# Eight more seven-product pairs in the down projections of an fp32 decoder trunk

## The chip, the core and the metric

The kernel runs on one core of one Trainium2 chip. The metric is device time in microseconds (us) of one execution. A core has a matrix engine (PE), whose weight loads (PEld) run beside its matmuls, a vector engine (DVE), a scalar engine (ACT), a general engine (POOL), and a sync engine (SP) that here does nothing but start DMA transfers. The 16 DMA engines of the core are shared by all queues; a transfer is started by SP or by POOL.

## The reference, cut to what matters

The reference is a decoder trunk of two layers on 256 tokens with D = 2048, all in float32. Layer 0 mixes tokens with gated linear attention, layer 1 with block-sparse attention. Each is followed by the same channel mixer:

```python
def conv_ffn(x, norm_w, w_up, conv_w, conv_b, w_down):
    S = x.shape[1]
    h = rms_norm(x, norm_w) @ w_up                 # 2048 -> 2 x 5632
    hp = jnp.pad(h, ((0, 0), (CONV_WIDTH - 1, 0), (0, 0)))
    acc = conv_b
    for j in range(CONV_WIDTH):
        acc = acc + conv_w[j] * hp[:, j:j + S]     # causal depthwise conv, width 3
    a, u = jnp.split(acc, 2, axis=-1)
    return (jax.nn.silu(a) * u) @ w_down           # 5632 -> 2048
...
    for layer in range(DEPTH):
        ...                                        # h = h + token mixer
        h = h + conv_ffn(h, ffn_norm[layer], ffn_w_up[layer], ffn_conv_w[layer],
                         ffn_conv_b[layer], ffn_w_down[layer])
```

The change touches the up projection (`@ w_up`, with the convolution and the gate), and above all the down projection (`@ w_down`), in both layers.

## The kernel before, in words

**Products.** Every float32 weight tile is split into two reduced-precision parts, whi (a rounded copy, ACT, line 143) and wlo (the rest, DVE, line 145); the activations are split in the same way. A product is three matmul passes: hi by hi, lo by hi, hi by lo.

**The weight stream.** `WeightStream` brings the weights once, as "halves" of 128 x 1024 floats (512 KB). SP starts each load (line 109) into one of 10 raw buffers (names wraw and ahead); ACT and DVE turn a half into one of 4 whi and 4 wlo buffers; PE uses it. In the down projections loads are started at most 10 halves ahead of the split, in the up projections 7. A raw buffer comes free when its half has been split.

**Up projection.** 22 groups of 8 steps, a step being one half and 12 matmuls. Behind each group ACT, DVE and POOL transpose the result, apply the convolution and the gate and split the hidden rows (`turn_up`, `conv`, `gate`). Some operand sums are made here too (below), and `make_ahead` forms sums of down-projection weights ahead of time: it loads two halves of w_dn into two raw buffers, does four DVE additions, and POOL stores both to DRAM ("parked" in tsum, line 339). It does so every 9 steps.

**Down projection.** `down` (lines 820 to 890) walks over two column blocks b of 1024 output columns. In each it takes 22 pairs; a pair is 256 of the 5632 hidden rows. The order of the pairs in a block is written out by hand in `ORDERS`, a table of one string for each layer and block; block 0 of both layers has the string `FIRST`. A plain number is a regular pair: two halves, eight products, 24 matmuls. A number with + or ^ is a seven-product pair, a Strassen-like scheme: 21 matmuls in place of 24. It needs sums of weights and sums of hidden rows as operands. Its weights come as one half of 256 KB, one of 512 KB and two parked halves of 512 KB, 1792 KB in all; with ^ the parked halves are loaded into long-lived slots (name sums) of the pool `big`, which has 32 slots, instead of the raw buffers. The last regular pairs of a block are its tail. Before, 58 pairs of 88 have seven products: 13 in block 0 of both layers, 15 and 17 in block 1 of layers 0 and 1.

**Operand sums of hidden rows.** A seven-product pair needs four sums ("combinations") of its hidden rows, each split in two; three of them are 384 KB. They are kept in `big` slots called comb; one slot has four quarters, so that three slots hold a fourth pair's sums in their last quarters. Three ways lead there: pairs 1 and 3 (EARLY) are made in the up projection and stay; the seven pairs of ASIDE are made in the up projection and put aside to DRAM (`put_aside`, lines 743 to 749, stored by POOL, line 748), and fetched back by POOL (`take_back`, line 751, DMA line 753) in block 0 of the down projection; the other pairs' sums are made in the down projection by DVE and ACT (`combine_parts`, line 755: one 128 x 512 addition, four 128 x 128 additions and the splits, lines 436 and 437). `MADE` gives for each pair the place in the block's order at which it is fetched or made. A pair's sums made in block 0 serve block 1 as well.

**What sets the order.** Each engine works through its own queue in program order. SP's loads follow the order of the halves and wait for a free raw buffer; POOL's queue holds copies for the last up-projection groups, then the fetches, then reloads of the residual stream (h, line 983, in layer 0; res, line 936, in layer 1).

Of the kernel before, what the change touches and what calls it, by code (L numbers as in the profile page):

```python
# [37 lines left out]
def _order(text):  # L38
# [117 lines left out]
def trunk(ctx: ExitStack, tc: tile.TileContext, xT, cst, msk, w1p, w2a, w_k, w_qa, w_v2, w_v, w_gt, w_g, w_got, w_go,  # L156
# [14 lines left out]
    def slot(shape, dt, name):  # L171
        return big.tile(shape, dt, name=name, tag="slot")
# [287 lines left out]
    make_ahead(0, w_dn0, 24, 9)  # L460
# [244 lines left out]
    combos, rooms_of = {}, {}  # L705
# [3 lines left out]
    def room(k, hid_k, kept):  # L709


        n = len(combos)
        if n % 4 < 3:
            rooms.append(slot([128, 4, 2, 128], F32R, "comb"))
            combos[k] = [(rooms[-1][:, f, 0], rooms[-1][:, f, 1]) for f in range(3)]
        else:
            combos[k] = [(c[:, 3, 0], c[:, 3, 1]) for c in rooms[-3:]]
        combos[k].append((hid_k[:, 0, 128:S], hid_k[:, 0, S + 128:]) if kept else
                         (rooms[-1][:, 3, 0], rooms[-1][:, 3, 1]))
        return rooms[-1] if n % 4 < 3 else None  # L720
# [99 lines left out]
    def down(layer, hid, ready, jobs):  # L820

        sevens = [{k for k, seven in order if seven} for order in ORDERS[layer]]
        done = set(EARLY)
        for b, order in enumerate(ORDERS[layer]):
            new = [k for k, seven in order if seven and k not in done]
            done |= set(new)
            todo = dict(jobs.get(b, {}))
            for k in MADE:
                if k not in new:
                    continue  # L830
                kept = k in sevens[-1]
                at, lag = MADE[k] if isinstance(MADE[k], tuple) else (MADE[k], 0)
                if lag:
                    todo.setdefault(at, []).append(
                        lambda k=k, kept=kept: rooms_of.update({k: room(k, hid[k], kept)}))
                todo.setdefault(at + lag, []).append(
                    (lambda k=k: take_back(layer, k, hid[k])) if k in ASIDE else
                    (lambda k=k, kept=kept: combine_parts(k, hid, kept)))
# [289 lines left out]
    make_ahead(1, w_dn1, 6, 9)  # L1128
# [157 lines left out]
```

## Time and profile before

| | us |
|---|---|
| median of three runs | 2169.53 |
| lowest and highest | 2169.51 and 2169.84 |
| the profiled execution, its own time | 2170.52 |
| its span (first to last instruction) | 2168.8 |
| PE busy in the span | 2160.1 |
| DVE, ACT, POOL busy | 1749.0, 1535.0, 351.5 |

Times inside the trace run from the span's start. The down projections lie, roughly, at 865 to 974 and 974 to 1092 us (layer 0, blocks 0 and 1) and at 1946 to 2055 and 2055 to 2165 us (layer 1); the up projections at 385 to 865 and 1466 to 1946 us. The share of the DMA engines is a mean over the 16 of the time that packets were under way; the GB/s beside it is what they moved. The granted clock of PE shows 9 (90% or more of 2.4 GHz) in all 40 slices of the page.

### The profile page before, as it was taken

Reading aid. Unit: us, or ns where it says so; the run is one execution under the profiler, and the core shown is the slowest. Engines: PE = TensorE matmul, PEld = TensorE weight load, DVE = VectorE, ACT = ScalarE, POOL = GpSimd, SP = SyncE. Lnnn points to the kernel's source line nnn. Section 1 sums busy time; section 2 is a strip of 40 time slices with the busy share of each in tenths; the row PEclk is TensorE's granted clock in tenths of the full one; section 3 lists DMA queues with packets and bytes.
Section 4 is the critical chain, followed back from the end, with each engine's and each line's share of the span. In section 5 each row is a group of like instructions: output and inputs, shape, how many; then the busy total and the mean of one; then the engine's idle time right before and its main releaser. Section 6 shows DMA issues by size and latency. Waiting matters only on the chain.

```text
span 2168.8 us, 30105 instructions
## 1 busy us (share of the span) xinstructions
PE 2160.1 (100%) x9936; PEld 1801.4 (83%) x9936; DVE 1749.0 (81%) x2525; ACT 1535.0 (71%) x2448; POOL 351.5 (16%) x519
## 2 busy tenths in 40 slices
PE   9999999999999999999999999999999999999999
PEld 7888888888888888888888888888888888888887
DVE  7676788778788887988977787587887888779898
ACT  6655554698899886767656575456888898967575
POOL 0000347100000004300002343150000000043000
PEclk9999999999999999999999999999999999999999
DMA  9586678978888886897968898779888888869996
GB/s 333 192 280 211 233 270 268 338 261 274 295 279 302 289 274 205 317 338 273 403 215 283 278 311 288 249 236 317 276 292 299 283 299 293 269 202 337 335 355 259
DMA packets 193600, 613.11 MB, mean 283 GB/s; under 512 B 38257, under 2 KB 38785, under 8 KB 193442
## 3 DMA queue, kind: packets, MB, share of 16 engines
q1 hardware_dynamic: 166322, 523.78, 71.1%
q0 software_dynamic: 26400, 86.60, 10.7%
q8 instruction: 78, 1.28, 0.2%
q10 hardware_dynamic: 720, 0.79, 0.1%
q14 instruction: 80, 0.66, 0.1%
HBM read 535.31 MB, written 75.78 MB: 282 GB/s over the span
## 4 chain that ended last, share of the span: by engine, by line
PE 99%; DMA 0%; DVE 0%; POOL 0%; issue 0%; SPq 0%; ACT 0%; POOLq 0%
PE acc L385 46%; PE acc L388 23%; PE acc L857 15%; PE p L857 6%; PE acc L370 5%; PE acc L372 2%; DMA wraw<-w_v 0%; PE sT L607 0%; PE tr L1059 0%; PE s L1077 0%; PE z L513 0%; PE o L493 0%; PE s L1075 0%; PE oT L493 0%; DVE wlo L145 0%; PE oT L492 0%
## 5 line engine op out<-in xcount | busy, mean ns | idle before, releaser
L145 DVE TENSOR_TENSOR wlo<-wraw,whi 128x1024 fp32r<-128x1024 f32 (+1 forms) x788 | 927.3, 1188 | 316.9 <-ACT whi L143 267.0
L143 ACT CAST whi<-wraw 128x1024 fp32r<-128x1024 f32 (+1 forms) x788 | 792.1, 1015 | 445.8 <-PE acc L385 262.5
L385 PE MATMUL acc<-whi,xw 128*128 128x512 f32 x3520 | 873.9, 390 | 1.4 <-ACT whi L143 1.2
L385 PEld LDWEIGHTS acc<-whi,xw 128*128 128x128 f32 x3520 | 659.7, 188 | 138.5 <-ACT whi L143 1.6
L388 PE MATMUL acc<-wlo,xw 128*128 128x512 f32 x1760 | 472.3, 389 | 0.0
L388 PEld LDWEIGHTS acc<-wlo,xw 128*128 128x128 f32 x1760 | 330.2, 188 | 68.4
L398 ACT COPY up<-uT 32x256 f32<-32x256 f32 x608 | 245.4, 404 | 8.5 <-DVE uT L776 1.0
L339 POOL DMA_DIRECT2D tsum<-ahead x116 | 62.6, 540 | 967.0 <-DVE ahead L327 563.5
L857 PE MATMUL acc<-whi,hid 128*128 128x512 f32 x588 | 167.6, 390 | 0.0
L145 DVE TENSOR_TENSOR wlo<-ahead,whi 128x1024 fp32r<-128x1024 f32 x98 | 120.5, 1232 | 17.4 <-ACT whi L143 11.1
L143 ACT CAST whi<-ahead 128x1024 fp32r<-128x1024 f32 x98 | 102.5, 1053 | 41.3 <-PE acc L857 19.8
L385 PE MATMUL acc<-whi,xkv 128*128 128x512 f32 x512 | 129.7, 391 | 0.0
L857 PEld LDWEIGHTS acc<-whi,hid 128*128 128x128 f32 x588 | 110.1, 188 | 22.6
L857 PE MATMUL p<-whi,hid 128*128 128x512 f32 x356 | 112.1, 389 | 0.0
L385 PEld LDWEIGHTS acc<-whi,xkv 128*128 128x128 f32 x512 | 95.3, 188 | 18.9
L857 PE MATMUL acc<-whi,comb 128*128 128x512 f32 x348 | 101.3, 389 | 0.0
L857 PE MATMUL acc<-wlo,hid 128*128 128x512 f32 x294 | 96.2, 389 | 0.0
L789 ACT ACTIVATE au<-up,cs 128x256 f32<-128x256 f32 x176 | 95.7, 593 | 0.0
L398 POOL COPY up<-uT 32x256 f32<-32x256 f32 x96 | 72.2, 752 | 96.4 <-DVE uT L776 74.1
L796 DVE SCALAR_TENSOR_TENSOR au<-up,cs,au 128x254 f32<-128x254 f32 x176 | 80.7, 483 | 0.0
L326 DVE TENSOR_TENSOR ahead<-ahead 128x512 f32<-128x512 f32 x116 | 80.2, 691 | 0.0
L327 DVE TENSOR_TENSOR ahead<-ahead 128x512 f32<-128x512 f32 x116 | 79.7, 687 | 0.1
(283 smaller groups left out, 2409.2 us busy)
## 6 DMA issues: line engine op xcount, KB each, us to landing
wraw<-w_up SPq DMA_DIRECT2D x352, 512.0 KB, 5.9
wraw<-w_dn SPq DMA_DIRECT2D x118, 512.0 KB, 6.4
ahead<-w_dn SPq DMA_DIRECT2D x116, 512.0 KB, 6.1
tsum<-ahead POOLq DMA_DIRECT2D x116, 512.0 KB, 6.1
ahead<-tsum SPq DMA_DIRECT2D x98, 512.0 KB, 6.1
wraw<-w_mq SPq DMA_DIRECT2D x32, 512.0 KB, 5.9
wraw<-w_kk SPq DMA_DIRECT2D x32, 512.0 KB, 6.3
wraw<-w_kv SPq DMA_DIRECT2D x32, 512.0 KB, 5.7
```

Source lines behind the costliest of these rows:

```text
L143: self.high = nc.scalar.copy(hi[:, a:b], src[:, a:b])
L145: self.low = nc.vector.tensor_sub(lo[:, a:b], src[:, a:b], hi[:, a:b].bitcast(F32))
L326: jobs = [lambda: V.tensor_sub(b22, b22, b12), lambda: V.tensor_sub(b12, b12, b11), lambda: V.tensor_add(b11, b22, b11), lambda: V.tensor_ ...
L327: lambda: V.tensor_add(b11, b22, b11), lambda: V.tensor_sub(b21, b21, b11)]
L339: nc.gpsimd.dma_start(parked[layer][at][:, o:o + 1024], t)
L370: T.matmul(ps[:, b, :], two[i][0][:, c:c + 128], xs(kt), start=kt == 0, stop=False)
L385: T.matmul(ps[:, t, :], xs(kt)[:, x0 + 128 * t:x0 + 128 * t + 128], hi[:, c:c + 512], start=kt == 0 and x0 == 0, stop=False)
L388: T.matmul(ps[:, t, :], xs(kt)[:, 128 * t:128 * t + 128], lo[:, c:c + 512], start=False, stop=kt == KT - 1)
L398: copy(y[32 * c:32 * c + 32, :, :, 32 * m:32 * m + 32], xs_[:, :, :, c])
L789: A.activation(au[:, i, :], t[:, i, :], AF.Identity, bias=col(cb + n), scale=col(cw + 2 * 2 * FT + n))
L796: V.scalar_tensor_tensor(au[:, i, 2:], t[:, i, :S - 2], col(cw + n), au[:, i, 2:], op0=OP.mult, op1=OP.add)
L857: T.matmul(p[n], x[xi], w[wi][:, 512 * f:512 * f + 512], start=n not in begun, stop=left[n] == 0)
```

## The change

The tables are new: 66 pairs have seven products (16 in block 0 of both layers, 16 and 18 in block 1), in other orders. Twelve pairs instead of seven have their operand sums put aside in each up projection, pairs 5 to 16, one in each of twelve groups in a row. Four of them (`TWICE`: 5, 6, 7, 9) are fetched in both blocks, each time into a `big` slot of its own (name comb3), so that the slot is free between. The others are fetched once. Where a fetched pair's sums lie in the fourth quarters of three slots, the fetch is three DMAs of 128 x 256. In layer 0 pairs 17 and 19 are still made in the down projection, in layer 1 pairs 17, 19, 18 and 4 (before: six and eight pairs). `make_ahead` works every 8 steps instead of 9. Lines move by 2 or 3 in the new program (109 becomes 111, 398 becomes 400, 753 becomes 756, the pieces are 759).

```diff
-ASIDE = (5, 7, 9, 11, 13, 15, 16)
-MADE = {5: 0, 17: (1, 4), 7: 1, 9: 2, 11: 3, 19: (4, 4), 13: 5, 15: 6, 16: 7, 12: 9, 14: 11, 10: 8, 8: 10, 18: 6, 6: 4}
-FIRST = "0 1+ 2 3+ 4 5+ 7+ 6 9+ 11+ 8 13+ 15+ 10 16+ 17+ 18 19+ 12+ 14+ 20 21"
+ASIDE = (5, 6, 7, 8, 9, 10, 11, 12, 13, 14, 15, 16)
+TWICE = (5, 6, 7, 9)
+FIRST = "0 1+ 3+ 2 5+ 7+ 9+ 4 6+ 11+ 8+ 13+ 18 15+ 10+ 16+ 17+ 12+ 19+ 14+ 20 21"
...
-ORDERS = [[_order(FIRST), _order("0 2 4 6 1+ 3+ 5+ 7+ 9+ 11+ 13+ 18 15^ 14+ 16+ 17^ 19+ 12^ 10+ 8^ 20 21")],
-          [_order(FIRST), _order("0 1+ 3+ 5+ 2 7+ 9+ 11+ 4 13^ 15+ 16+ 17^ 6+ 18^ 19+ 12^ 14+ 10^ 8+ 20 21")]]
+ORDERS = [[_order(FIRST), _order("0 2 4 18 1+ 3+ 11+ 8+ 13+ 15^ 10+ 16+ 5+ 7+ 17^ 9+ 6+ 19+ 12^ 14+ 20 21")],
+          [_order(FIRST), _order("0 1+ 3+ 11+ 8+ 13^ 15+ 2 10+ 16^ 5+ 7+ 17^ 9+ 6+ 19+ 12^ 14+ 18+ 4^ 20 21")]]
+BEGIN = {5: 0, 7: 1, 9: 2, 6: 3, 11: 5, 8: 6, 13: 7, 17: 8, 15: 9, 10: 10, 19: 11, 16: 11, 12: 13, 14: 15}
+MADE = [[BEGIN, {5: 7, 7: 8, 9: 10, 6: 11}], [BEGIN, {5: 5, 7: 6, 9: 8, 6: 9, 18: 11, 4: 13}]]
...
-    make_ahead(0, w_dn0, 24, 9)
+    make_ahead(0, w_dn0, 24, 8)
...
+        if k in TWICE:
+            own = slot([128, 3, 2, 128], F32R, "comb3")
...
     def take_back(layer, k, hid_k):
-        own = room(k, hid_k, True)
-        nc.gpsimd.dma_start(own[:, 0:3].rearrange("a b c d -> a (b c d)"), aside[layer, ASIDE.index(k)])
+        own = room(k, hid_k)
+        kept = aside[layer, ASIDE.index(k)]
+        if own is not None:
+            nc.gpsimd.dma_start(own[:, 0:3].rearrange("a b c d -> a (b c d)"), kept)
+        else:
+            for f, c in enumerate(rooms[-4:-1]):
+                nc.gpsimd.dma_start(c[:, 3].rearrange("a c d -> a (c d)"), kept[:, 256 * f:256 * f + 256])
...
-    make_ahead(1, w_dn1, 6, 9)
+    make_ahead(1, w_dn1, 6, 8)
```

In the whole program PE has 9012 matmuls of 512 columns after the change and had 9036. DMAs started by POOL go from 255 to 311 (16 more stores of parked sums, 10 more stores of operand sums, 30 more fetches), those started by SP from 1101 to 1133. DVE has 2565 instructions instead of 2527, ACT 2429 instead of 2423.

SP's queue of loads, as it enters block 0 of layer 0, before (two wraw of 128x1024 are a regular pair; 128x512, 128x1024 and two ahead are a seven-product pair):

```order
L109 DMA wraw<-w_dn 128x1024 x2
L109 DMA wraw<-w_dn 128x512
L109 DMA wraw<-w_dn 128x1024
L109 DMA ahead<-tsum_81 128x1024 x2
L109 DMA wraw<-w_dn 128x1024 x2
L109 DMA wraw<-w_dn 128x512
L109 DMA wraw<-w_dn 128x1024
L109 DMA ahead<-tsum_81 128x1024 x2
L109 DMA wraw<-w_dn 128x1024 x2
L109 DMA wraw<-w_dn 128x512
L109 DMA wraw<-w_dn 128x1024
L109 DMA ahead<-tsum_81 128x1024 x2
```

The same place after the change:

```order
L111 DMA wraw<-w_dn 128x1024 x2
L111 DMA wraw<-w_dn 128x512
L111 DMA wraw<-w_dn 128x1024
L111 DMA ahead<-tsum_81 128x1024 x2
L111 DMA wraw<-w_dn 128x512
L111 DMA wraw<-w_dn 128x1024
L111 DMA ahead<-tsum_81 128x1024 x2
L111 DMA wraw<-w_dn 128x1024 x2
L111 DMA wraw<-w_dn 128x512
L111 DMA wraw<-w_dn 128x1024
L111 DMA ahead<-tsum_81 128x1024 x2
```

Two seven-product pairs now follow each other where a regular pair stood between them, and after the next regular pair come three in a row.

POOL's queue at the change from up to down projection of layer 1, before (comb<-aside is a fetch, COPY the last up-projection groups):

```order
L748 DMA aside<-aside 128x768
L398 COPY up<-uT 32x8x32 x32
L753 DMA comb<-aside 128x768
L398 COPY up<-uT 32x8x32 x16
L753 DMA comb<-aside 128x768 x6
L936 DMA res<-hscr 128x512 x8
```

The same place after the change, to the end of block 0's fetches:

```order
L400 COPY up<-uT 32x8x32 x16
L756 DMA comb_18401<-aside 128x768
L756 DMA comb_18461<-aside 128x768
L756 DMA comb_18520<-aside 128x768
L756 DMA comb<-aside 128x768
L759 DMA comb<-aside 128x256
L756 DMA comb<-aside 128x768
L759 DMA comb<-aside 128x256 x2
L756 DMA comb<-aside 128x768
L759 DMA comb<-aside 128x256 x2
L931 DMA res<-hscr 128x512 x4
```

and behind these, in the same queue:

```order
L756 DMA comb<-aside 128x768 x2
L759 DMA comb<-aside 128x256 x2
L756 DMA comb_19634<-aside 128x768
L756 DMA comb_19681<-aside 128x768
L756 DMA comb_19764<-aside 128x768
L756 DMA comb_19811<-aside 128x768
L931 DMA res<-hscr 128x512 x4
```

Where six fetches stood behind the last copies there are now eight whole ones in block 0 with seven small pieces among them (two more pieces stand further up the queue, in the up projection); four residual loads stand ahead of the last two whole ones; and four re-fetches (the numbered names of the last fence) come for block 1.

## Rows read from the trace of the kernel before

**Rows 1.** The page's part 4: chain that ended last, share of the span.

```profile
PE 99%; DMA 0%; DVE 0%; POOL 0%; issue 0%; SPq 0%; ACT 0%; POOLq 0%
```

**Rows 2.** Waits of PE, whole span: us in total, times, longest.

```profile
PE acc L385 <- ACT whi L143: 1.5, 2, 1.2
PE junk L215 <- POOL idle L212: 1.3, 1, 1.3
PE tr L1059 <- DVE q L1051: 1.1, 1, 1.1
PE acc L388 <- DVE wlo L145: 0.7, 1, 0.7
PE acc L385 <- DVE xw L258: 0.2, 1, 0.2
```

**Rows 3.** Timeline of PE, layer 0, block 0: start us, us, instruction.

```profile
903.37 0.62 PE L857 MATMUL acc<-whi,hid 128*128 128x512 f32 x2
...
906.09 0.62 PE L857 MATMUL acc<-whi,hid 128*128 128x512 f32 x2
```

**Rows 4.** Windows: us; busy PE, PEld, DVE, ACT, POOL; clock, DMA share, GB/s.

```profile
883.00:913.00 30.00, 30.00 (x134) 24.86 (x133) 29.54 (x51) 23.11 (x36) 3.84 (x7) 1.00 1.04 384
913.00:965.00 52.00, 52.00 (x231) 43.06 (x230) 44.41 (x55) 35.41 (x45) 0.00 (x0) 1.00 0.91 325
1018.00:1083.00 65.00, 65.00 (x289) 53.81 (x288) 60.30 (x72) 47.92 (x57) 2.14 (x4) 1.00 1.02 404
1966.00:1995.00 29.00, 29.00 (x130) 24.02 (x129) 28.54 (x49) 23.25 (x36) 2.28 (x5) 1.00 1.05 388
2088.00:2097.00 9.00, 9.00 (x42) 7.44 (x41) 9.00 (x14) 7.26 (x9) 0.54 (x1) 1.00 0.96 311
2097.00:2145.00 48.00, 48.00 (x214) 39.75 (x213) 43.57 (x55) 35.76 (x45) 1.61 (x3) 1.00 1.03 404
1666.00:1766.00 100.00, 100.00 (x443) 82.82 (x442) 84.73 (x137) 90.64 (x168) 5.31 (x10) 1.00 0.88 299
```

**Rows 5.** DMA issues, 883 to 900 us: KB each, median us to landing.

```profile
comb<-aside POOLq DMA_DIRECT2D x6, 384.0 KB, 9.8
```

**Rows 6.** Timeline of POOL: fetches of layer 0, last residual load of layer 1, block 0.

```profile
883.66 3.18 POOL L753 DMA_DIRECT2D comb<-aside  x6
...
2005.09 0.54 POOL L936 DMA_DIRECT2D res<-hscr  x1 [2.01 <-DVE hid L437]
```

**Rows 7.** DMA issues of 886.3–886.7, 1967.3–1967.7, 1047.2–1048, 2121–2121.4 us.

```profile
wraw<-w_dn SPq DMA_DIRECT2D x1, 256.0 KB, 10.5
...
wraw<-w_dn SPq DMA_DIRECT2D x1, 256.0 KB, 9.8
...
wraw<-w_dn SPq DMA_DIRECT2D x1, 512.0 KB, 10.7
...
wraw<-w_dn SPq DMA_DIRECT2D x1, 256.0 KB, 9.6
```

**Rows 8.** Timeline of PE where these four halves are first used.

```profile
901.11 0.61 PE L857 MATMUL acc<-whi,hid 128*128 128x512 f32 x2
...
1981.99 0.61 PE L857 MATMUL acc<-whi,hid 128*128 128x512 f32 x2
...
1062.59 0.62 PE L857 MATMUL acc<-whi,hid 128*128 128x512 f32 x2
...
2134.31 0.62 PE L857 MATMUL acc<-whi,hid 128*128 128x512 f32 x2
```

**Rows 9.** Timeline of ACT shortly before the last of them.

```profile
2130.12 1.05 ACT L143 CAST whi<-ahead 128x1024 fp32r<-128x1024 f32 x1 [1.13 <-DMA ahead<-tsum]
```

**Rows 10.** Lines of DVE by form, up projection of layer 0: count, busy, mean ns.

```profile
L326 DVE TENSOR_TENSOR ahead<-ahead 128x512 f32<-128x512 f32 x34 | 23.2, 683 | 0.0
...
L437 DVE TENSOR_TENSOR aside<-comb,aside 128x384 fp32r<-128x384 f32 x7 | 3.9, 550 | 0.0
L725 DVE TENSOR_TENSOR comb<-au 128x128 f32<-128x128 f32 x9 | 2.6, 292 | 0.3
```

More of the change, by code (lines that the diff above doesn't have):

```diff
@@ L703, in project, with room @@
             after(2, n.close)
-    combos, rooms_of = {}, {}
+    combos = {}
     rooms = []
     aside = dram.tile([2, len(ASIDE), 128, 768], F32R, name="aside")
-    def room(k, hid_k, kept):
-        n = len(combos)
+    def room(k, hid_k):
+        n, in_hid = len(rooms), (hid_k[:, 0, 128:S], hid_k[:, 0, S + 128:])
+        if k in TWICE:
+            own = slot([128, 3, 2, 128], F32R, "comb3")
+            combos[k] = [(own[:, f, 0], own[:, f, 1]) for f in range(3)] + [in_hid]
+            return own
         if n % 4 < 3:
             rooms.append(slot([128, 4, 2, 128], F32R, "comb"))
[L715 to L720, printed above, removed]
+            combos[k] = [(rooms[-1][:, f, 0], rooms[-1][:, f, 1]) for f in range(3)] + [in_hid]
+            return rooms[-1]
+        combos[k] = [(c[:, 3, 0], c[:, 3, 1]) for c in rooms[-3:]] + [in_hid]
+        rooms.append(None)
     def sums(halves_):
@@ L729, in sums, with combine @@
         return t
-    def combine(k, hid_k, halves_, kept=True):
-        own = room(k, hid_k, kept) if k not in combos else rooms_of[k]
+    def combine(k, hid_k, halves_):
+        own = room(k, hid_k)
         t = sums(halves_)
-        if own is not None and not kept:
-            return split(own[:, :, 0], own[:, :, 1], t)
         if own is not None:
@@ L751, in take_back, with combine_parts @@
     def take_back(layer, k, hid_k):
-        own = room(k, hid_k, True)
-        nc.gpsimd.dma_start(own[:, 0:3].rearrange("a b c d -> a (b c d)"), aside[layer, ASIDE.index(k)])
-    def combine_parts(k, hid, kept):
+        own = room(k, hid_k)
+        kept = aside[layer, ASIDE.index(k)]
[4 more added lines that the diff above has]
+                nc.gpsimd.dma_start(c[:, 3].rearrange("a c d -> a (c d)"), kept[:, 256 * f:256 * f + 256])
+    def combine_parts(k, hid):
         t = temp("whole")
@@ L758, in combine_parts @@
             V.tensor_add(t, hid[k][:, :, :S], hid[k][:, :, S:])
-        combine(k, hid[k], [(t[:, i, :128], t[:, i, 128:]) for i in range(2)], kept)
+        combine(k, hid[k], [(t[:, i, :128], t[:, i, 128:]) for i in range(2)])
     def ffn(layer, nrm, then):
@@ L764, in ffn @@
         combos.clear()
+        rooms.clear()
         cw = C_CW + layer * 3 * 2 * FT
@@ L820, in down @@
     def down(layer, hid, ready, jobs):
-        sevens = [{k for k, seven in order if seven} for order in ORDERS[layer]]
-        done = set(EARLY)
         for b, order in enumerate(ORDERS[layer]):
[L825 to L838, printed above, removed]
+            todo = {i: list(jobs_) for i, jobs_ in jobs.get(b, {}).items()}
+            for k, at in MADE[layer][b].items():
+                todo.setdefault(at, []).append(
+                    (lambda k=k: take_back(layer, k, hid[k])) if k in ASIDE else (lambda k=k: combine_parts(k, hid)))
             low = acc_ps.tile([128, 2, 512], F32, name="acc")
```

## The prediction

> **What bounds the kernel now.** I read the chain of waits first: 99% of it is PE [rows 1], so the time is a row of matmuls. The list of PE's waits comes next: five kinds, 4.8 us in all, of which [rows 2] show the four larger; none is at a line of the down projection, so there PE never stands. The timeline then gives its pace: from 903.37 to 906.09 us PE starts 12 matmuls [rows 3], 2.72 us or 0.227 us each. A matmul less is 0.227 us less, as long as weights, parts and operand sums still arrive in time. How near they are to being late is read from the windows by stretch [rows 4] and from four transfers followed from issue to use [rows 7, 8].
>
> In the windows the DMA share is 1.02 to 1.05 in most of the down projections, at 384 to 404 GB/s: full, and 404 GB/s is what it holds over 65 and over 48 us. So DMA runs beside PE with little to spare, and the question is whether the cushion lasts.
>
> The cushion at its thinnest: in layer 0, block 0 a 256 KB half issued at 886.5 lands 10.5 us later, at 897.0 [rows 7], and PE uses it at 901.11 [rows 8]: 4.1 us. In between ACT must cast it; a full cast takes 1.05 us [rows 9], so about 3.05 us are left. The other blocks in the same way: layer 1, block 0: 1967.5 + 9.8 = 1977.3, use 1981.99, left 3.6. Layer 0, block 1: 1047.4 + 10.7 = 1058.1, use 1062.59, left 3.4. Layer 1, block 1: 2121.2 + 9.6 = 2130.8, use 2134.31, left 2.5. In this last one ACT already stands 1.13 us for a parked half [rows 9]. The windows of issue are 0.4 to 0.8 us wide, so each is good to some 0.3 us.
>
> **The change part by part.** *Matmuls.* Eight pairs turn from 24 matmuls to 21, in all 24 fewer: 24 x 0.227 = -5.45 us, all on the path.
>
> *Up projections.* Five more pairs per layer are put aside there, and parked sums come every 8 steps. On DVE one put-aside is four sums of 0.29, a split of 0.55 and one of about 0.29: 2.0 us [rows 10]. A group of 8 steps lasts 8 x 2.72 = 21.8 us. DVE is busy 84.7 of 100 us and ACT 90.6 in the middle of layer 1's [rows 4]; about every second group there holds a put-aside, now each does: half of 2.0 in 21.8 adds 4.6 points to DVE. Four additions of 0.683 us [rows 10] per 8 steps instead of 9 add 12.5 - 11.1 = 1.4 points. DVE comes to some 91%, ACT to some 92: both fit on average, and PE is the cover. The rhythm is the new risk: 8 steps is the length of a group, so the parked sums always meet the same phase of convolution, gate and put-aside. The nearest row for such a collision is PE's longest wait for a cast, 1.2 us [rows 2]; once per layer it is 2.4, and below zero it can't go, as no wait of size stands there to be removed. Bounds 0 to 2.4; I take 1.0.
>
> *DMA in the down projections.* A seven-product pair moves 1792 KB, 1.835 MB: 4.54 us at 404 GB/s, against 21 x 0.227 = 4.77 us of PE; it saves up only 0.23 us. A regular pair moves 1.049 MB, 2.60 us, against 5.45: it saves up 2.85. So the regular pairs are what refills the cushion, and each exchange costs it 0.786 MB (1.95 us) and 0.68 us in which PE is earlier: 2.63 us. A fetch of 384 KB is 0.393 MB, 0.97 us; the three pieces of 128 x 256 together are as much. Neither fetches nor sums cost PE anything themselves; they share the 16 engines, and that is visible: the six fetches issued from 883.66 on [rows 6] take 9.8 us to land [rows 5].
>
> - Layer 0, block 0: the same burst of six stays at the entry. Up to the thin place stand one exchange (2.63) and 0.655 MB more fetched (a fetch and two pieces, 1.62): 3.05 - 4.25 = -1.2, the cushion is gone. From there to the regular pair 18, which now stands behind four sevens, come fetches of 0.393 and 0.655 MB and two reloads of h moved up (0.524 MB), together 3.9 us, against four sevens' savings of 0.9: another 3.0. All of it on the path: 4.2. In the trace this later stretch ran at 325 GB/s and a share of 0.91 [rows 4], so it isn't full today. Bounds 0 to 4.2; I take 2.5.
> - Layer 1, block 0: 3.6 - 4.25 = -0.65, then fetches of 2.6 us against 0.9: all of it 2.3. The residual loads stand ahead of the last two fetches in POOL's queue; the last of them was issued at 2005.09 us [rows 6], 59 us into the block, while the pairs behind (16, 12) come at places 15 and 17, over 70 us in: hidden, and if that cover went, a fetch of some 10 us would be late by what is missing. I take 1.5.
> - Layer 0, block 1: one exchange (2.63) and four re-fetches (1.57 MB, 3.9 us) in a stretch that is full today, 404 GB/s over 65 us [rows 4], with no regular pair between the first and the last seven: 3.4 - 6.5 = -3.1. Bounds 0 to 3.1; I take 2.5, near the upper, since no row shows room there.
> - Layer 1, block 1: the same exchange and re-fetches, 2.5 - 6.5 = -4.0, but the re-fetches come early in the block, and 2088 to 2097 us ran at 311 instead of 404 GB/s [rows 4], room for 0.84 MB or 2.1 us: -1.9. Bounds 0 to 1.9; I take 1.0, the middle.
>
> *Operand sums no longer made in the down projections.* Eight combinations go from DVE and ACT there. DVE was busy 29.54 of 30 and 28.54 of 29 us at the entry of the two block 0s [rows 4], and 9.00 of 9 in layer 1, block 1. But PE waited nowhere for it, so nothing is gained on the path; and more sevens bring more splitting per microsecond, which takes most of it back at the entries. Zero. If DVE should still be late there, it shows as PE waiting for wlo, at most in the place of the waits counted above.
>
> *POOL.* 56 more DMA issues at 0.53 us (3.18 us for six, [rows 6]) are 30 us of an engine with 351.5 busy of 2168.8: hidden.
>
> The trace speaks for one price of DMA: 404 GB/s where the share is over 1.0 [rows 4]. The Trainium skill, "DMA: Bandwidth & Descriptors", section "Specifications", gives a fabric ceiling of 435 GB/s and about 358 GB/s as HBM's limit per core. By 435 a seven-product pair would need 4.22 us and save up 0.55, and the full count of the first block above would be 2.4 us (an estimate from that page); by 358 a pair would need 5.13, lose 0.36 each time, and the count would be 7.5. The trace keeps under the ceiling and goes well over the 358: it held 404 for 65 us.
>
> *Sum.* -5.45 + 1.0 + 2.5 + 1.5 + 2.5 + 1.0 = +3.05. The profiled execution took 2170.52 us (span 2168.8 and 1.7 around it), so 2173.6 by its own clock; it stands 1.0 above the median of 2169.53. Against the median: 2172.6.
>
> **The rivals.**
> *A, the cushions suffice.* The waits stay at nothing and the change is worth its matmuls: 2169.53 - 5.45 = 2164.1. For it: PE waits nowhere in the down projections today, transfers start up to ten halves ahead, and the share falls to 0.91 and 311 GB/s in places. Against it: four thin places of 2.5 to 3.6 us, and more than that is taken from each.
> *B, the bytes decide.* DMA can't catch up, and each block pays its full count: 4.2 + 2.3 + 3.1 + 1.9, and 2.4 in the up projections, 13.9 in all: 2178.0, slower. The place is the rows of sevens without a regular pair between; the price 2.63 us for an exchange and 0.97 for a fetch; it decides from where the fetches and exchanges up to a place pass its cushion plus 5.45/4 us, 1.4 per block. For it: 1.02 to 1.05 of DMA share. Against it: a wait of PE early in a block gives the transfers time, so that later places need less.
> *C, fetches starve behind DVE.* If POOL couldn't issue while DVE is busy, the five or so fetch issues added to each block 0's first half would each hold the path 0.53 us: 5 x 0.53 x 2 = 5.3 on top of the forecast, 2177.9. Against it: the six issues took 3.18 us [rows 6] in a stretch where DVE had 0.46 us idle in 30 [rows 4], so they ran beside it. The rule is in the Trainium skill, "SBUF — State Buffer", section "SBUF: two separate sides": a DMA from POOL's queue can't get its descriptors written while DVE holds the port they share. The trace shows no sign of it.
> That the change doesn't do what it says I exclude: the program has 24 matmuls less.
>
> **How the numbers follow.** The forecast, part of the count on the path: 0.52, with a range of its own from 2166 to 2176. A: 0.13. B: 0.30, up to 2180, since the up projections may cost more than one wait per layer. C: 0.03; the last 0.02 for something unseen. What a measurement can tell from no change is 0.2%, 4.3 us: faster is under 2165.2, slower over 2173.9. Faster gets A and a little of the forecast's lower end, 0.14. Slower gets B but for its mildest part, C, and the upper quarter of the forecast: 0.42. No change 0.44. The range 2165.3 to 2179.5 leaves out most of A and the tail of B, 2 in 10.
>
> **What would show it.** Right: 21 matmuls per exchanged pair, with PE's pace still 0.227 us; in the list of PE's waits new rows at line 852 (before 857) for whi, wlo or, behind them, ACT waiting for wraw and ahead, at about 25 to 60 us into block 0 of both layers and 35 to 60 us into block 1 of layer 0; a DMA share of 1.0 with no dip through these stretches; waits of 7 to 9 us in all. Wrong: no waits of PE at that line (A), or waits of 12 us and more (B); PE waiting for comb instead of weights, which would put the fetches' order or their slots in the dock; or a wait of over 3 us in the up projections, where I count one.

## The result, and the profile after

| | median us | runs | lowest to highest | ratio to before (95% interval) |
|---|---|---|---|---|
| before | 2169.49 | 6 | 2169.33 to 2169.84 | |
| after | 2188.10 | 6 | 2184.59 to 2190.90 | 1.0085 [1.0072, 1.0098] |

The change makes the kernel 18.6 us slower; 2172.6 was forecast, with a range to 2179.5. Its runs also spread over 6 us, where those of before agree within 0.5. The profiled execution took 2187.4 us (span 2185.6).

PE's waits over the whole span (us in total, times, longest), which answer to [rows 2]:

```profile
PE acc L852 <- ACT whi L145: 5.0, 9, 1.8
PE p L852 <- ACT whi L145: 2.3, 2, 1.7
PE tr L1054 <- DVE q L1046: 1.5, 1, 1.5
PE acc L387 <- DVE go L439: 1.3, 2, 1.2
```

and those of PE's weight loads, which [rows 2] do not hold:

```profile
PEld acc L852 <- ACT whi L145: 13.7, 22, 2.2
PEld acc L387 <- ACT whi L145: 8.1, 22, 1.5
PEld p L852 <- ACT whi L145: 3.5, 3, 2.1
```

The down projections (L852) now wait for whi, as forecast, but so does L387, a line that the up projections and most other products share: 22 small waits that the list of PE hardly shows, since a matmul waits for its weight load. Eighteen of them lie in the up projection of layer 0 (386 to 870 us), where the list of PE has none:

```profile
PEld acc L387 <- ACT whi L145: 5.3, 18, 0.5
```

Where the time went is seen best by stage. The table gives the time from PE's first 512-column matmul of a stage to the first of the next in the trace; b0 and b1 are the blocks of a down projection. Each b1 ends at the start of the projection's last matmul; in layer 0, matmuls of the next stage run ahead among those of b1 and are counted there. In brackets the matmuls of that kind, where a kernel has another count than the row above.

| profiled run of | to up, layer 0 | up 0 | b0, layer 0 | b1, layer 0 | between | up 1 | b0, layer 1 | b1, layer 1 |
|---|---|---|---|---|---|---|---|---|
| before | 384.3 | 479.3 | 110.8 (489) | 115.7 (502) | 375.1 (1485) | 479.3 | 110.8 (489) | 107.9 (476) |
| after | 385.9 | 482.4 | 114.3 (480) | 118.5 (497) | 376.9 (1487) | 479.3 | 115.2 (480) | 107.6 (473) |
| e1_no_fetch | 386.0 | 482.3 | 109.0 | 115.2 (494) | 381.0 (1490) | 479.3 | 113.0 | 107.2 |
| e2_every_9 | 384.1 | 481.2 | 119.3 | 118.0 (497) | 374.9 (1487) | 483.0 | 119.2 | 108.4 |
| e3_phase | 384.6 | 485.6 | 112.5 | 118.6 | 379.0 | 479.3 | 114.5 | 107.6 |
| e4_sp_fetch | 385.8 | 482.4 | 110.3 | 116.0 | 380.4 | 479.3 | 112.7 | 107.9 |
| e5_rhythm | 384.3 | 479.3 | 114.8 | 118.1 | 374.3 | 479.3 | 113.8 | 108.0 |
| e6_regular | 385.6 | 480.9 | 111.9 (489) | 117.9 | 380.6 | 479.3 | 111.5 (489) | 107.3 |
| e7_sp_rhythm | 384.1 | 479.3 | 110.1 (480) | 116.1 | 374.3 | 479.3 | 113.0 (480) | 108.1 |
| e8_res_late | 384.3 | 479.3 | 112.4 | 116.3 | 374.3 | 479.3 | 119.1 | 107.2 |
| e9_ten_regular | 384.2 | 479.3 | 110.1 (483) | 116.1 (500) | 374.3 | 479.3 | 112.2 (483) | 109.3 (476) |
| e10_ten_late | 384.2 | 479.3 | 110.1 | 117.5 (497) | 374.5 | 479.3 | 112.3 | 108.3 (473) |
| e11_regulars_first | 384.5 | 479.3 | 114.5 (480) | 116.0 | 374.3 | 479.3 | 118.3 (480) | 108.2 |
| e12_regulars_ten | 384.6 | 479.3 | 109.8 (483) | 115.9 (500) | 374.3 | 479.3 | 110.8 (483) | 109.0 (476) |

With 0.227 us for each matmul less, after stands longer than its matmuls ask for by 1.6 (to the up projection), 3.2 (up 0), 5.5, 4.0, 1.3 (between), 0, 6.4 and 0.4 us: 22.4 in all, less 5.45 of matmuls, is the 16.9 by which the stages grew (spans: 16.8).

In the up projection of layer 0 the loss begins late. These are the windows of after there, columns as in [rows 4]:

```profile
386.00:708.00 322.00, 322.00 (x1428) 266.51 (x1427) 269.10 (x429) 272.27 (x493) 24.95 (x47) 1.00 0.86 300
708.00:862.00 154.00, 153.72 (x669) 123.95 (x668) 132.72 (x208) 127.71 (x225) 31.00 (x47) 1.00 0.81 279
```

PE keeps its pace in the first; in the second it does 669 matmuls where before does 681 in as long. Measured group by group in the trace, groups 14 to 20 of the 22 each take 0.2 to 0.5 us longer than PE needs, and no group from the third to the thirteenth does. What happens ahead of that is that ACT's lead is used up: the shortest time from the end of a half's cast to its first matmul falls from 3.0 us in group 8 to 0.1 in group 14, about half a microsecond a group.

The windows of after by stretch, columns as in [rows 4]:

```profile
869.00:887.00 18.00, 18.00 (x81) 14.93 (x80) 17.01 (x23) 14.57 (x21) 12.28 (x15) 1.00 0.54 182
887.00:903.00 16.00, 16.00 (x71) 12.90 (x70) 15.97 (x22) 12.09 (x18) 7.21 (x13) 1.00 0.98 335
903.00:927.00 24.00, 21.08 (x88) 15.51 (x86) 18.05 (x25) 14.16 (x18) 3.21 (x6) 1.00 1.09 399
1052.00:1059.00 7.00, 5.89 (x18) 4.46 (x19) 4.43 (x5) 4.86 (x6) 0.00 (x0) 0.76 1.03 406
1979.00:2015.00 36.00, 33.62 (x141) 25.64 (x140) 30.89 (x44) 25.11 (x35) 8.44 (x16) 1.00 1.07 384
```

In the first row of layer 0's block 0 DMA is half idle; then POOL gets free of its copies and starts the fetches (timeline of POOL; x4 is the number of instructions):

```profile
888.43 2.12 POOL L756 DMA_DIRECT2D comb<-aside  x4
890.51 0.56 POOL L759 DMA_DIRECT2D comb<-aside  x1
891.03 0.57 POOL L756 DMA_DIRECT2D comb<-aside  x1
891.55 1.11 POOL L759 DMA_DIRECT2D comb<-aside  x2
```

and what was issued from 887 to 910 us lands late (KB each, median us to landing; [rows 5] had 9.8 for a fetch):

```profile
ahead<-tsum SPq DMA_DIRECT2D x7, 512.0 KB, 12.3
wraw<-w_dn SPq DMA_DIRECT2D x6, 512.0 KB, 11.2
comb<-aside POOLq DMA_DIRECT2D x8, 384.0 KB, 12.4
comb<-aside POOLq DMA_DIRECT2D x7, 128.0 KB, 14.4
```

From 903 on the share is 1.09 and PE works 21.08 of 24 us. ACT's waits there name DMA first (903 to 930 us):

```profile
ACT whi L145 <- DMA wraw<-w_dn: 4.6, 7, 1.3
ACT whi L145 <- DVE wlo L147: 2.8, 2, 1.6
ACT whi L145 <- PE acc L852: 2.4, 4, 1.0
ACT whi L145 <- DMA ahead<-tsum: 2.0, 3, 1.0
```

So there are two losses: a DMA backlog in the down projections, and something ahead of them that is no matter of the down projections at all.

### The profile page after: what moved, and what is told of

Same layout as the page of the kernel before. It is cut to its first block, busy times and chain, and to the rows that moved or that the text cites. A ratio compares the mean times of both kernels' runs of the same rounds, so it can differ in the third digit from the quotient of the medians.

```text
span 2185.6 us, 30357 instructions
## 1 busy us (share of the span) xinstructions
PE 2167.0 (99%) x9912; PEld 1794.1 (82%) x9912; DVE 1788.2 (82%) x2563; ACT 1544.8 (71%) x2454; POOL 388.2 (18%) x575
## 4 chain that ended last, share of the span: by engine, by line
PE 92%; DMA 5%; DVE 1%; ACT 1%; issue 1%; POOL 0%; SPq 0%; ACTq 0%; DVEq 0%; POOLq 0%
PE acc L387 45%; PE acc L390 22%; PE acc L852 11%; PE acc L372 5%; PE p L852 4%; DMA wraw<-w_dn 3%; PE acc L374 2%; DMA ahead<-tsum 1%; DVE wlo L147 1%; DMA wraw<-w_v 0%; ACT whi L145 0%; PE sT L609 0%; ACT up L400 0%; PE tr L1054 0%; DMA wraw<-w_kv 0%
## 5 line engine op out<-in xcount | busy, mean ns | idle before, releaser
L387 PE MATMUL acc<-whi,xw 128*128 128x512 f32 x3520 | 876.0, 390 | 1.6 <-ACT whi L145 1.1
L387 PEld LDWEIGHTS acc<-whi,xw 128*128 128x128 f32 x3520 | 657.8, 188 | 143.2 <-ACT whi L145 7.4
L341 POOL DMA_DIRECT2D tsum<-ahead x132 | 71.3, 540 | 868.4 <-DVE ahead L329 418.6
L852 PE MATMUL acc<-whi,hid 128*128 128x512 f32 x572 | 164.7, 393 | 4.1 <-ACT whi L145 3.9
L147 DVE TENSOR_TENSOR wlo<-ahead,whi 128x1024 fp32r<-128x1024 f32 x116 | 142.3, 1233 | 25.4 <-ACT whi L145 21.6
L145 ACT CAST whi<-ahead 128x1024 fp32r<-128x1024 f32 x116 | 121.5, 1052 | 56.4 <-PE acc L852 21.3
L852 PEld LDWEIGHTS acc<-whi,hid 128*128 128x128 f32 x572 | 106.1, 188 | 31.1 <-ACT whi L145 10.0
L387 PE MATMUL acc<-whi,xkv 128*128 128x512 f32 x512 | 129.9, 391 | 0.0
L852 PE MATMUL acc<-whi,comb 128*128 128x512 f32 x396 | 119.2, 394 | 1.2 <-ACT whi L145 1.1
L387 PEld LDWEIGHTS acc<-whi,xkv 128*128 128x128 f32 x512 | 95.2, 188 | 18.9
L852 PE MATMUL p<-whi,hid 128*128 128x512 f32 x308 | 100.1, 391 | 2.3 <-ACT whi L145 2.3
L328 DVE TENSOR_TENSOR ahead<-ahead 128x512 f32<-128x512 f32 x132 | 93.0, 705 | 8.8 <-DMA ahead<-w_dn 7.6
L852 PE MATMUL acc<-wlo,hid 128*128 128x512 f32 x286 | 94.8, 392 | 0.1
L329 DVE TENSOR_TENSOR ahead<-ahead 128x512 f32<-128x512 f32 x132 | 92.7, 703 | 0.0
L852 PEld LDWEIGHTS acc<-whi,comb 128*128 128x128 f32 x396 | 74.5, 189 | 19.0 <-ACT whi L145 3.7
```

The source lines that it names most:

```text
L145: self.high = nc.scalar.copy(hi[:, a:b], src[:, a:b])
L147: self.low = nc.vector.tensor_sub(lo[:, a:b], src[:, a:b], hi[:, a:b].bitcast(F32))
L328: jobs = [lambda: V.tensor_sub(b22, b22, b12), lambda: V.tensor_sub(b12, b12, b11), lambda: V.tensor_add(b11, b22, b11), lambda: V.tensor_ ...
L329: lambda: V.tensor_add(b11, b22, b11), lambda: V.tensor_sub(b21, b21, b11)]
L341: nc.gpsimd.dma_start(parked[layer][at][:, o:o + 1024], t)
L387: T.matmul(ps[:, t, :], xs(kt)[:, x0 + 128 * t:x0 + 128 * t + 128], hi[:, c:c + 512], start=kt == 0 and x0 == 0, stop=False)
```

## The experiments

Each kernel was timed 4 to 11 times beside the kernel before on the same chip. The theory was: the down projections lose to a backlog that the fetches make, the rest is lost to the new rhythm of the parked sums. Medians are of the timed runs, stages those of the table. The length of a block comes from one profiled run alone and is good to some 2 us: block 0 of layer 0, which is the same in e7 and e8, took 110.1 and 112.4.

**e1_no_fetch.** Its edit:

```diff
     def take_back(layer, k, hid_k):
+        combos[k] = combos[1][:3] + [(hid_k[:, 0, 128:S], hid_k[:, 0, S + 128:])]
+        return
```

> Left out: every fetch of operand sums; the fetched pairs multiply the sums of pair 1 in their place. All else, the matmuls and the weight loads too, stays as in the changed kernel. Theory: the stalls of the down projections are a DMA backlog that the fetches make (12 of 0.39 MB in each block 0, issued within 20 us, and 4 more in each block 1). The trace of the changed kernel puts the excess over its matmuls at 5.5 us (layer 0, block 0), 4.0 (layer 0, block 1), 6.4 (layer 1, block 0) and 0.4. Without fetches these go to under 2 us in sum: about 2188 - 14 = 2174 us, and no wait of PE for whi in the down projections. Rival 1: the weight bytes of the seven-product pairs alone outrun DMA (each pair 4.54 of 4.77 us at 404 GB/s): at least 8 us stay, 2182 or more. Rival 2: DVE's and ACT's splits are the late part: nothing changes beyond 2 us.

Measured: 2181.2 us, ratio 1.0052 [1.0039, 1.0065], where about 2174 was expected. The stalls of the blocks fall by 5.2, 2.6, 2.2 and 0.4 us: without fetches 0.3 us is left in layer 0's block 0, but 4.2 in layer 1's. That last number does not say what the fetches cost there, for the edit does more than it is meant to: it leaves the `big` slots of the fetched sums free, and loads of block 1's parked halves that wait for such slots (those of the ^ pairs) move forward into block 0 of layer 1. Issues of that block, first after, then e1:

```profile
sums<-tsum SPq DMA_DIRECT2D x1, 512.0 KB, 9.5
...
sums<-tsum SPq DMA_DIRECT2D x6, 512.0 KB, 11.3
```

Five halves more are 2.6 MB, 6.5 us at 404 GB/s, issued from 1998 to 2006 us. The total disappoints also because the stage between the layers is longer, 381.0; there PE stood 4.2 us at once for an ACT result in this run. My theory holds for layer 0's block 0; for layer 1's this run can't tell it from its rivals.

**e2_every_9**

```diff
-    make_ahead(0, w_dn0, 24, 8)
+    make_ahead(0, w_dn0, 24, 9)
-    make_ahead(1, w_dn1, 6, 8)
+    make_ahead(1, w_dn1, 6, 9)
```

> The changed kernel with parked sums made every 9 steps, as before the change. Theory: the 8-step rhythm costs what was lost outside the down projections: 3.2 us in the up projection of layer 0 and 3.4 in the two stages ahead of the up projections (1.6 and 1.8). With 9 these go back: about 2188 - 6 = 2182 us; the down projections may get up to 1 us worse, as a set or two of sums falls into block 0. Rival: the loss there is from the five more put-asides and their stores, not from the rhythm: the up projection of layer 0 keeps its 3 us, and only the two earlier stages can gain, 2185 to 2188.

Measured: 2194.7 us, 1.0115 [1.0101, 1.0129]: slower than after. The two stages ahead did go back (384.1 and 374.9), the up projections didn't (481.2; 483.0, where after had lost nothing), and the block 0s lost 4 to 5 us more. The window of the entry of layer 0's block 0 (866 to 884 us, columns as above) shows what is new there:

```profile
866.00:884.00 18.00, 16.32 (x73) 13.18 (x72) 14.33 (x21) 13.14 (x20) 11.02 (x18) 1.00 0.95 347
```

A set of sums is still being made there, in two raw buffers, with 2 MB to and fro: PE stands already where it had its longest cushion. I had priced that at 1 us. The 8 steps are what gets 66 sets done in time.

**e3_phase**

```diff
-    make_ahead(0, w_dn0, 24, 8)
+    make_ahead(0, w_dn0, 28, 8)
```

> The changed kernel with the first set of parked sums of layer 0 begun 4 steps later (28 instead of 24), still every 8. Theory: not how often but at which step of a group the sums fall decides: layer 1, which starts at another step, loses nothing in its up projection. The up projection of layer 0 gains most of its 3.2 us, the stage ahead of it changes by under 1.5: 2184 to 2186. Rival (density): sums every 8 steps are too many wherever they fall: no gain, 2187 to 2189.

Measured: 2189.8 us, 1.0092 [1.0076, 1.0107]. The up projection of layer 0 got worse, 485.6. So the same density costs 3.2 at one step of the group, 6.3 at another, and 0 in layer 1, which has a third. Density alone is refuted, phase is not; but the direction was a miss. Nor is it phase alone: with 9 steps, which cost before nothing, e2 lost 1.9 and 3.7 us in the up projections, so the put-asides, now in twelve groups in a row, most likely have a part in it. Counted from the first step of an up projection, the sets began at step 0 of a group in after's layer 0, at 4 here, at 6 in layer 1.

**e4_sp_fetch** (the pieces likewise; `bitcast` only renames the type, the bytes are the same)

```diff
-            nc.gpsimd.dma_start(own[:, 0:3].rearrange("a b c d -> a (b c d)"), kept)
+            with tc.issue_after(ws.load.ins):
+                nc.sync.dma_start(own[:, 0:3].rearrange("a b c d -> a (b c d)").bitcast(F32), kept.bitcast(F32))
```

> The changed kernel with all fetches started by SP, each behind the weight load that was last put in its queue at that place, instead of by POOL. The same bytes. In the changed kernel POOL issues the first fetches of block 0 only at 888 us, behind the copies of the last up-projection group, all twelve by 909 us, while from 869 to 887 us DMA runs at 182 GB/s and a share of 0.54. Theory (burst): with the fetches begun in that idle time and spread over the block, the stalls of the two block 0s fall by half or more: 2188 - 6 = 2182 us or less. Rival (bytes): the total decides, the stalls only move: 2186 to 2190. Rival (queue): a fetch that waits for its slot holds up SP's loads behind it: slower, up to 2195.

Measured: 2182.5 us, 1.0057 [1.0045, 1.0070]. With the same bytes the block 0s fall by 4.0 and 2.5 us, block 1 of layer 0 by 2.5. DMA at the entry and behind it, as in the first and third windows of after:

```profile
869.00:887.00 18.00, 18.00 (x81) 14.89 (x80) 17.14 (x23) 14.35 (x21) 12.40 (x15) 1.00 0.67 220
...
903.00:927.00 24.00, 24.00 (x106) 19.59 (x106) 21.93 (x29) 16.24 (x20) 1.09 (x2) 1.00 1.02 395
```

Some of the bytes moved into the idle time, and PE works 24 of 24 us from 903 to 927. It was the burst more than the bytes. There is no sign that SP's queue is the cheaper one: from 887 to 903 and from 903 to 927 us DMA moves 331 and 395 GB/s here, 335 and 399 in after. What the stage between lost (380.4) hides part of the gain.

**e5_rhythm**

```diff
         for i, at in enumerate(ahead[layer]):
-            after(first + every * i, lambda at=at: work(at))
+            after(first + 9 * i if i < n else turns + 8 * (i - n), lambda at=at: work(at))
```

with `n` all sets but the last 21, and `turns` 126 in both layers, two steps ahead of the first step of the up projection (step 6 of a group).

> The changed kernel with another timetable for the parked sums alone: ahead of the up projections every 9 steps (from 24 in layer 0, from 6 in layer 1, as before the change), in the up projections every 8 steps, in both layers at the 6th step of a group, which is where the changed kernel's layer 1 has them and loses nothing in its up projection. The last set is out before the down projection begins. Theory (phase): the up projection of layer 0 goes from 482.4 to 479.3 us, the stage ahead of it and the one between the layers lose their 1.6 and 1.8: 2188 - 6.5 = 2181.5 us, with the down projections as they are. Rival: density or the put-asides cost it, whatever the step: the up projection of layer 0 keeps 2 us or more, 2185 to 2188.

Measured: 2178.5 us, 1.0039 [1.0026, 1.0052], 3 less than expected. Every stage outside the down projections is back at 384.3, 479.3, 374.3 and 479.3 us, and the runs agree within 2 us. The gain, 9.6 us, is 3.5 more than the profile of after had lost there; in four of the kernels with 8 steps all through (e1, e3, e4, e6) the stage between took 379 to 381 us, so after's profiled run was a mild one. Why the step matters shows in ACT's waits from 706 to 860 us. After:

```profile
ACT au L809 <- DVE au L803: 12.6, 7, 2.2
ACT hid L438 <- DVE au L811: 5.3, 8, 1.0
ACT whi L145 <- PE acc L387: 3.6, 5, 1.6
```

e5_rhythm:

```profile
ACT whi L145 <- PE acc L388: 13.5, 22, 1.7
...
ACT au L810 <- DVE au L804: 2.7, 2, 1.7
ACT hid L439 <- DVE au L812: 2.1, 2, 1.5
```

In after ACT waits with the gate (L809) for DVE's convolution, 12.6 us in all, and the casts of the weights that follow the gate in its queue come late; it hardly waits for PE any more, which is to say it has no lead. With the sums at another step it waits for PE, 13.5 us in all, and DVE had no less to do (busy 135.2 us from 706 to 860, in after 132.7 from 708 to 862). The shortest lead, which fell to 0.1 us in after, stays at 4.6 in groups 3 to 20.

**e6_regular** (6, 8 and 10 of `FIRST` without their +)

> The changed kernel with pairs 6, 8 and 10 of block 0 as regular pairs in both layers (they multiply what lies in their place, so their rows are not the right ones; their three parked sums are neither made nor loaded), but with all fetches as in the changed kernel. Adds 9 matmuls per block 0, 2 x 2.04 us. Theory (backlog from both): three exchanges are worth 3 x 2.63 = 7.9 us of DMA per block, more than the 5.5 and 6.4 us of stalls: the block 0s stand for under 1 us each, 110.9 to 112 us long instead of 114.3 and 115.2, the whole about 2188 - 3.4 - 4.4 = 2180 us, somewhat less with six sets fewer to make. Rival (burst alone): the twelve fetches within 20 us make the stalls by themselves: at least 3 us stay in each block 0, 2185 or more.

Measured: 2180.9 us, 1.0055 [1.0042, 1.0068]. The block 0s take 111.9 and 111.5 us, 1.1 and 0.6 more than before with as many matmuls: the full burst of fetches makes nearly no stall when three exchanges are undone. Fetches or exchanges alone fit (e1 in layer 0, and this); both together don't.

**e7_sp_rhythm**: e4 and e5 together.

> The fetches by SP (as in the run that did that alone, 2182.5 us) and the timetable of parked sums of the run above together. If the two causes are apart, their gains add: 2182.5 - 3.1 in the up projection - 1.5 and up to 4.8 in the stages ahead: 2173 to 2178 us, still above the kernel before, since layer 1's block 0 keeps its 3.9 us and block 1 of layer 0 1.5. If the stalls outside the down projections are a matter of luck from run to run: about 2180.

Measured: 2173.4 us over 11 runs, 1.0015 [1.0006, 1.0024]. The gains add. The blocks still lose 1.3, 1.5, 4.2 and 0.9 us, 7.9 against 5.45 of matmuls.

**e8_res_late**

```diff
-                    nc.gpsimd.dma_start(x, hscr[...])
+                    with tc.issue_after(ws.load.ins):
+                        nc.sync.dma_start(x, hscr[...])
```

> The one above, with the residual loads of layer 1 (4 of 256 KB in each block) also started by SP, behind the weight load that is last in its queue when the block's sevens end, instead of by POOL as soon as a buffer is free (1992 to 2012 us in the changed kernel, in its full stretch). Theory: these 1.05 MB (2.6 us at 404 GB/s) are why layer 1's block 0 keeps 3.9 us where layer 0's keeps 1.5: it falls by 2 us or more, to 2171 to 2175 us in all. Rival: it is the same backlog of weights and fetches, and a load put into SP's queue only delays those behind it: no gain, or 1 to 2 us more.

Measured: 2177.4 us, 1.0034 [1.0022, 1.0047]. A new wait came in its place (PE's waits from 1950 us on):

```profile
PE acc L855 <- DVE u L904: 6.0, 1, 6.0
PE acc L855 <- ACT whi L145: 1.0, 1, 1.0
```

The residual lands too late for the sums that free PE's accumulators. Without these 6.0 us the block would take 113.1, what e7 took: no sign that the residual loads are what holds layer 1 back. As this profile is 2.3 us slower than e7's in a block that the edit doesn't touch, a gain of that size could be hidden.

**e9_ten_regular** (pair 10 without + in all four orders, out of `ASIDE` and `BEGIN`) and **e10_ten_late** (the same in `FIRST` alone; in block 1 pair 10 is made at place 6 and 4)

> Fetches by SP and the timetable of parked sums by phase (together 2173.4 us), and pair 10 regular in both blocks of both layers, so not put aside nor fetched: 62 seven-product pairs. Costs 12 matmuls, 2.7 us. Theory (bytes): the four blocks still stand 1.3, 1.5, 4.2 and 0.9 us, all with DMA at 401 to 406 GB/s; an exchange undone gives 2.63 us and a fetch 0.97, so the stalls go to about 0.5 in all: 2173.4 - 7.4 + 2.7 = 2168.7 us, at or just under the kernel before. Rival: the remaining waits are from the order in which loads stand in SP's queue, not from the bytes: they stay above 4 us, 2172 or more.

> As the run beside it, but pair 10 regular in block 0 alone; in block 1 it has seven products, its sums made there by DVE and ACT: 64 seven-product pairs, 1.4 us of matmuls more than 66. Theory (bytes): the block 0s lose their stalls (1.3 and about 3.6 of 4.2 us), the block 1s keep theirs: 2173.4 - 4.9 + 1.4 = 2169.9 us. Rival: making the sums in block 1 makes DVE late there, where it is busy 90% and more: 2 us or more worse than that.

Measured: 2172.2 us, 1.0009 [1.0000, 1.0018], and 2172.7, 1.0013 [1.0004, 1.0021]. Both theories miss, and both times are those of the rivals. In e10 block 1 of layer 0 stands 3.0 us over its matmuls, where e7's stood 1.5. And with fewer bytes layer 1's block 0 still takes 112.2, 2.7 us over its matmuls. Its stall stands at 1998 to 2001 us, behind this stretch of e9:

```profile
1964.00:1980.00 16.00, 16.00 (x71) 12.99 (x70) 15.97 (x23) 14.52 (x21) 0.55 (x1) 1.00 0.96 330
1980.00:2000.00 20.00, 19.30 (x82) 14.87 (x82) 16.65 (x23) 11.66 (x14) 1.62 (x3) 1.00 1.03 393
```

DVE is busy all of the first 16 us, and DMA runs below its ceiling. My reading was that the halves are split late, so buffers come free late. That does not explain why layer 1 is the slower one: the same stretch of layer 0 in e9 looks the same, and its block loses 0.6 us.

```profile
884.00:900.00 16.00, 16.00 (x71) 12.95 (x70) 15.97 (x24) 14.57 (x21) 0.00 (x0) 1.00 0.96 325
```

What does differ is the bytes: in e7 block 0 of layer 1 moves 40.8 MB, that of layer 0 40.0, since it has 1.05 MB of residual loads and a parked half of block 1 where layer 0 reloads 0.52 MB of h. The 0.9 MB are 2.2 us at 404 GB/s (an estimate), of the 2.9 us that lie between the two stalls. No run separates the two readings.

**e11_regulars_first** (e7 with `FIRST = "0 2 4 18 1+ 3+ 5+ 7+ 9+ 6+ 11+ 8+ 13+ ..."`) and **e12_regulars_ten** (e9 with `"0 2 4 1+ 3+ 18 5+ 7+ 9+ 6+ 11+ 10 8+ 13+ ..."`)

> Fetches by SP and the timetable by phase (2173.4 us), with block 0's regular pairs at its beginning in both layers: 0 2 4 18, then sixteen sevens. The same matmuls and bytes. In the run it starts from, DVE is busy 16.0 of 16 us from 20 to 36 us into block 0 and DMA runs there at only 315 to 333 GB/s, though PE's cushion shrinks; after that DMA runs at 401 to 406. Theory (DVE at the entry): the last groups' convolution and the splits of three and a half halves a pair fill DVE there, so raw buffers come free late and loads start late; a regular pair has two halves to split in 5.4 us. With regulars first the cushion stays whole until DVE is free: the block 0s lose 1 us (layer 0) and 3 us (layer 1), 2169 to 2170 us. Rival (bytes): a row of 16 sevens with the fetches is 34 MB, 84 us at 404 GB/s against 76 us of PE, and the cushion can't carry 8 us: stalls late in block 0, 2174 to 2178.

> As the 62-pair kernel (pair 10 regular in both blocks, 2172.2 us), with block 0 as 0 2 4 1+ 3+ 18 and then sevens, pair 10 among them. The same matmuls and bytes as that kernel. Theory (DVE at the entry): its block 0s still stand 0.7 and 2.8 us; with three regulars at the entry they stand under 0.5 each: 2172.2 - 2.5 = 2169.7 us, level with the kernel before. Rival (bytes): the stall moves to the later row of sevens and stays 2 us or more: 2172 to 2174.

Measured: 2180.7 us, 1.0049 [1.0037, 1.0062], and 2171.5, 1.0008 [0.9999, 1.0017]. With all regulars first DVE is relieved, but DMA, which should gain if DVE held it up, runs still slower, and the row of sixteen sevens pays. The windows of e11 in layer 1:

```profile
1964.00:1980.00 16.00, 16.00 (x72) 13.24 (x71) 11.24 (x17) 11.95 (x17) 1.15 (x3) 1.00 0.75 252
...
2000.00:2020.00 20.00, 18.65 (x75) 15.27 (x76) 16.85 (x25) 14.43 (x19) 1.08 (x2) 0.91 1.03 400
```

With three at the entry and two in the row (e12) the block 0s come to 109.8 and 110.8, 0.3 and 1.3 us over their matmuls; 1.4 us less than e9 in layer 1 is within what one profile is good for. That is the best version found, and it can't be told from the kernel before: four pairs more with seven products than before, and the 2.7 us of matmuls are given back in stalls of 0.3, 0.7, 1.3 and 1.1.

## Why the prediction was wrong

Two steps failed. The count of DMA in the two block 0s was put at 2.5 and 1.5 us and measured 5.5 and 6.4; the new rhythm of the parked sums was put at 1.0 us, in the up projections alone, and measured 3.2 there and 2.9 in stages that the sum left out. Term by term:

- *Matmuls, -5.45.* Right: 24 less at an unchanged pace.
- *Up projections, 1.0, at most 2.4.* Wrong. The prediction saw the rhythm ("the parked sums always meet the same phase") and then bounded it by one wait of 1.2 us per layer, as if it struck once. A bad phase takes from ACT's lead in every group that has sums and a put-aside; PE stands only when the lead is gone, and from there on in every group: 18 waits, 3.2 us in layer 0, and none in layer 1. A trace in which the lead lasts has no wait from which that could be read. e3 and e5 show that with twelve put-asides the step decides. And the cost of a stage that the change also touches was left at nothing: the timetable of the sums starts ahead of the up projections, and 2.9 us went there in the profiled run, more in others (e5).
- *Layer 0, block 0: 2.5 of a full 4.2; layer 1, block 0: 1.5 of 2.3.* Measured 5.5 and 6.4. The mechanism was right, the sizes were not. The fetches were spread over the block by their places in `BEGIN` and only 1.62 us of them counted up to the thin place; but POOL runs ahead of PE and sends them off as soon as it and their slots are free: in after eight whole fetches and seven pieces in 21 us (one whole fetch and two pieces had gone earlier), as six went at once in [rows 6]. e4 shows what the burst costs: 4.0 and 2.5 us; e6 shows that with three exchanges undone the same burst costs 1.1 and 0.6. The price was 404 GB/s throughout, where [rows 4] had 384 and 388 at the two entries, with fetches among the loads, and after has 384 from 1979 to 2015 us. And taking half of a count because the trace had gaps elsewhere was no argument: three of the four blocks paid more than their full count, the fourth 0.4 of 1.9.
- *DVE's sums, 0, since "PE waited nowhere for it".* Open. In after's blocks the list of PE's waits names whi alone, so the sign that was named did not come; of ACT's waits from 903 to 930 us 2.8 of 11.8 us are for DVE's wlo. That a full DVE holds up the buffers in layer 1 was argued from e9, e11 and e12 and is not shown (above). Why layer 1's block 0 loses more than layer 0's stays open; e6 shows only that it, too, goes with the exchanges.
- *Layer 0, block 1: 2.5 of 3.1.* Measured 4.0; a slower clock is in it (below): 7 us at a granted clock of 0.76 are some 1.7 us of it (an estimate), so without it the term is near.
- *Layer 1, block 1: 1.0.* 0.4: right within its bounds.
- *The rivals.* B had the right mechanism and the wrong total, 2178.0; it was summed from the same short counts. The upper end of the range came from it. In the profiled runs its sum of 13.9 us stands against 22.4: outside the down projections 6.1 against 2.4 (1.6, 3.2 and 1.3 in three stages), in the blocks 16.3 against 11.5. The medians lie another 1.8 us further apart than the two profiled runs. C is not seen: in after POOL issues eight fetches and pieces in a row from 888.43 on at 0.53 us each while DVE is busy 15.97 of 16 us, and the whole ones land in 12.4 us where SP's loads take 11.2 to 12.3. Of the Trainium skill's rule on DVE and POOL's queue ("SBUF — State Buffer", "SBUF: two separate sides") this DVE work shows no sign.
- *The signs.* The prediction's own sign of being right, 7 to 9 us of waits of PE at line 852, came out: 5.0 and 2.3. It was a poor sign, for the blocks lost 16.3 us; the list of PE's weight loads has 17.2 us of waits for whi at that line.

What stays open is why the stage between the layers loses 1 to 5 us with 8 steps. e5 shows that the timetable does it, and the lists of PE's waits name the place: a matmul of the attention waits once for a value tile of ACT (PE o L492 for vm L485), 0.6 us in after, 4.2, 2.9, 2.3 and 4.2 in e1, e3, e4 and e6, and not at all in before, e5 or the kernels built on it. Why ACT is late there, and not always by as much, no run shows.

## What to carry to other kernels

Price a periodic job by its phase against the period of what it meets: what it takes from the lead per period, over all periods and every stage that it runs in, and not by the one worst wait of a trace in which it has another phase. Look for waits at the weight loads too, where PE's own list may show few. Where two streams share a saturated resource, ask when each is really issued (a queue that is not tied to the consumer sends everything at once) and price the mix at the rate that the trace shows for the mix. And when a cushion is overdrawn by your own count, don't halve the deficit without a row that shows the room; of four here, three cost more than the full count. Before an experiment that leaves something out is read, check what moves into the room that it makes (e1).

## What the runs showed of the hardware

A stall can cost more than it lasts. In after, PE stood at 1053 us for whi, and the matmuls behind it came slower (timeline of PE):

```profile
1053.05 1.20 PE L852 MATMUL acc<-whi,hid 128*128 128x512 f32 x4 [1.77 <-ACT whi L145]
1054.31 1.22 PE L852 MATMUL acc<-wlo,hid 128*128 128x512 f32 x2
1055.33 1.91 PE L852 MATMUL acc<-whi,comb 128*128 128x512 f32 x4
```

Four in 1.71 us (1055.33 to 1057.04) are 0.43 each instead of 0.227: the lower clock, 1.2 GHz, after a wait of 1.77 us; the granted clock of 1052 to 1059 us is 0.76. In this run that was the only stretch of 10 us under 0.99, though a wait of 1.67 us at 2009.83 us had no slower matmuls behind it; in e11 two waits of 2.2 us were each followed by the same pace, and in before there is none.
